# Order of the first loads, and of the MLP's products and weight sums, in a one-core hybrid decoder layer

## The chip, the cores and the metric

The kernel runs on one core of a Trainium2 chip. The metric is the device time of one launch in microseconds (us), lower is better; a time is the median of several runs. A core has five engines that work side by side and wait for each other by semaphores: TensorE (PE, matrix products; PEld is its loading of the stationary operand), VectorE (DVE), ScalarE (ACT), GpSimd (POOL) and SyncE (SP). SP, ACT and POOL also issue transfers between the chip's main memory and the on-chip memory.

## The reference

One layer: RMSNorm, one wide projection, two token mixers (pooling and a convolution) that are gated and summed, an output projection, and an MLP with a squared ReLU, all in float32.

```python
h = concat([meta, x])                       # 16 meta tokens, 256 tokens, width 2048
u = rms_norm(h, g_pre_mix)
z, v, g, gate_a, gate_b = split(u @ w_in)   # 1024, 1024, 1024, 2048, 2048 columns
y_a = multiscale_pool(z) @ w_pool_out
y_b = silu(layer_norm(depthwise_conv(v * sigmoid(g), 31 taps))) @ w_conv_out
m = sigmoid(gate_a) * y_a + sigmoid(gate_b) * y_b
h = h + rms_norm(m @ w_o, g_post_mix)
u = rms_norm(h, g_pre_mlp)
f = square(relu(u @ w_up)) @ w_down         # 2048 -> 8192 -> 2048
h = h + rms_norm(f, g_post_mlp)
return h[16:]
```

## The kernel before

**Products of split weights.** Every weight block of 1 MB (`raw`) is split into a high part, rounded by ACT (`hi`, L342, L801, L1755), and a low part, the rest, made by DVE (`lo`, L345, L806, L1760). A product takes three matmuls for each block of 128 rows (high x high, high x low, low x high). There are three buffers for high parts and three for low ones, so a weight can be split only when the product three places earlier is done. PE works through the products in a written order and never out of it.

**The start.** x lies in `x_in` (two tiles of 128 tokens), the meta tokens in `m_in`, and the first norm's weights `g_pre_mix` in 16 rows. Before anything is projected, the rows are transposed into columns (`rows_to_columns`, L407), the meta tokens are transposed in 16 pieces (`meta_tiles`, L483) and each 128 columns of x are transposed (`x_tile`, L473), scaled by ACT (L475) and split by DVE (L476). The first 512 columns of x come as two halves, one a tile, one issued by ACT and one by SP (L420). `LEAD` = 3 column blocks are turned before the first product (`acc_v`, L519). `keep_warm` (L436) fills PE with transposes of an identity whose result nobody reads: 13 ahead of the rows, 5 ahead of the first product. SP then issues the first weights in pieces, and x's further blocks between them (L337, L417).

**The MLP.** The 8192 hidden columns are done in eight pieces of 1024. Per piece there are eight products with `w_up`, called U with the half (0, 1), the pair (a, b) and the half of the depth (0, 1): U1a0 is one of them. They accumulate in banks u0 and u1, which ACT and DVE empty (`up_pair`, L1832, L1839) before relu, square and split (L1859 to L1911, tiles `F_raw` and `forms`). For `w_down`, the first seven pieces use Strassen's scheme in Winograd's form on 2 x 2 blocks: seven products P1 to P7 for one half of the output columns and seven, Q1 to Q7, for the other, in place of eight each. Four of each seven take a sum of weight blocks. P5, P6, P7 and P4 change the block B11 or B12 by adding another; Q5, Q6, Q7 and Q4 do the same with C. Before, P5, P6, Q5 and Q6 are summed by DVE from two loaded blocks (L1772, `SUM_FOR`), and P7, P4, Q7 and Q4 by a transfer that POOL issues and that adds a block from main memory onto the loaded one (L1777, `BROUGHT_FOR`). The last piece is done with eight plain products.

**Banks.** P1, P6, P7 and P4 use bank a; P5, P3 and P2 bank b; Q1, Q5, Q6 and Q7 bank x11 (its tile is `acc_up`); Q2, Q3 and Q4 have a bank each and keep their totals in it. After each of the others, `give` takes the bank's total: ACT in the first piece when it is the first to reach its place in the result (L1959), DVE otherwise (L1963). The next product in that bank waits for this.

**What sets the order.** `FIRST_PIECE`, `PIECE` and `LAST_PIECE` are strings that give PE's order of products; a + means that the product belongs to the next piece, R is a small step of the norm. A planner (`Plan`) takes the work of the other engines with assumed durations and orders each engine by due times that follow from PE's row; the order is fixed when the program is built. Seven 1 MB rooms hold loaded blocks, and `loads` issues the next load on SP whenever one is free.

Of the kernel before, what the change touches and what calls it, by code (L numbers as in the profile page):

```python
# [16 lines left out]
P = 128  # L17
# [24 lines left out]
SUMMED = {('gate0', 0): '67', ('gate0', 2): '57', ('gate1', 0): '5', ('co', 2): '46', ('o', 0): '46'}  # L42


class Plan:
# [151 lines left out]
def hybrid_block(ctx: ExitStack, tc: tile.TileContext, ins: dict, out: bass.AP):  # L197
# [217 lines left out]
    def load_x(b):  # L415
        sl = slice(b * CW, (b + 1) * CW)
        nc.sync.dma_start(x_in[:, :, sl], xv[:, :, sl])  # L417

    for t, queue in enumerate((nc.scalar, nc.sync)):
        queue.dma_start(x_in[:, t, :CW], xv[:, t, :CW])  # L420
# [139 lines left out]
    def turn_and_split(k):  # L560
        if k < KD:
            x_tile(k)
        if k == 0:
            meta_parts.pop(0)()
        pieces_to(k + 1)

    for k in range(LEAD):
        turn_and_split(k)
    keep_warm(DUMMIES[1])
    for k in range(KD):  # L570
        for j, acc in enumerate(accs):
            mm3(acc, *opened[k // HALF[0]][:2], u, (k % HALF[0], k), slice(j * P, (j + 1) * P),
# [66 lines left out]
    S1_z = Lazy("s1", [P, KP, L], "z")  # L639
# [22 lines left out]
    names_sums = [f"E{b}" for b in range(4)] + [f"O{b}" for b in range(3)]  # L662
    names_y = [f"yy{q}{l}" for q in range(KP) for l in ("", "l")]
    names_z = [f"z{q}" for q in range(KP)]
    names_s = [[f"S{b}{t}{n}" for t in range(NT) for n in range(NB)] for b in range(2)]
    names_sa = [f"sa{h}{l}" for h in range(2) for l in ("", "l")]
    names_o = [f"og{t}{n}" for t in range(NT) for n in range(NB)]
# [259 lines left out]
    def convolve(q0, nq):  # L927
        for q in on(q0, nq):
            on_scalar(T, lambda q=q: nc.scalar.activation(
                C_c()[:, q, :], A_a()[:, q, 0:T], AF.Identity, scale=taps[:, q, 0:1],  # L930
                bias=col("b_dw", q)), (f"a{q}", "taps", "vecs"), (f"c{q}",), 0.18)

        def tap(i):
            def f():
                for q in on(q0, nq):
                    nc.vector.scalar_tensor_tensor(  # L936
                        C_c()[:, q, :], A_a()[:, q, i:i + T], taps[:, q, i:i + 1], C_c()[:, q, :],
                        op0=ALU.mult, op1=ALU.add)
            return f
        for i in range(1, TAPS):  # L940
            plan.add("DVE", 0.4 * nq, tap(i), reads=[f"a{q}" for q in on(q0, nq)],
                     writes=[f"c{q}" for q in on(q0, nq)], late=0.1)

    def evac_z(q, bank):
        on_vector(L, lambda: nc.vector.tensor_mul(S1_z()[:, q, :], banks[bank][:, :L], rb),
                  (bank, "rb"), (f"z{q}",))

    def level(g):
# [6 lines left out]
    def pool(g):  # L955
        w = 1 << g
        lo_ = 2 * w - 1
        q0 = g * GK
        box = {}

        def add(j):
            def f():
                src = level(g - 1)[:, GK:, :] if g else S1_z()
                dst = level(g)
                q = j * GK
                nc.vector.tensor_add(dst[:, q:q + GK, lo_:], src[:, q:q + GK, lo_:],
                                     src[:, q:q + GK, lo_ - w:L - w])
            reads = [level_name(g - 1, j + 1)] if g else [f"z{q}" for q in on(j * GK, GK)]
            on_vector(GK * (L - lo_), f, reads, (level_name(g, j),))

        def diff():
            box["dm"] = dm = tmp.tile([P, GK, T], F32, tag="junk", bufs=1, name=f"dm_{g}")
            nc.vector.scalar_tensor_tensor(
                dm, level(g)[:, 0:GK, M:], 1.0 / (2 * w), S1_z()[:, q0:q0 + GK, M:],
                op0=ALU.mult, op1=ALU.subtract)

        def high():
            nc.scalar.copy(K0_d()[:, q0:q0 + GK, 0, :], box["dm"])

        def low():  # L980
            nc.vector.tensor_sub(K0_d()[:, q0:q0 + GK, 1, :], box["dm"],
                                 f32(K0_d()[:, q0:q0 + GK, 0, :]))
        for j in range((KP - q0) // GK):
            add(j)
            if j == 0:
                on_vector(GK * T, diff, [level_name(g, 0)] + [f"z{q}" for q in on(q0, GK)],
                          ("junk",))
                on_scalar(GK * T, high, ("junk",), (f"d{g}",))
                on_vector(GK * T, low, ("junk", f"d{g}"), (f"d{g}l",))
# [352 lines left out]
    def fu_step():  # L1342
        plan.take(form_names("fu"), names_d)
        names = [f"qu{t}{h}" for t in (1, 2) for h in (1, 2)]
        plan.take(["raw10"] + names, names_z)
# [340 lines left out]
        steps += [(s[:-1], i + 1) if s[-1] == "+" else (s, i) for s in text.split()]  # L1686
    products = [s for s in steps if s[0] != "R"]


    RAW_OF = {"1": "11", "5": "11", "6": "11", "4": "11", "3": "22", "7": "12", "2": "21"}  # L1690
    RAW_OF = {p + k: b + r for p, b in ("PB", "QC") for k, r in RAW_OF.items()}
# [161 lines left out]
    def relu_squared(h, pr, i, s_name, box):  # L1853
# [20 lines left out]
        if i < NP - 1 and h == 0:  # L1874
# [4 lines left out]
        elif i < NP - 1:  # L1879
# [11 lines left out]
        def src():  # L1891
# [5 lines left out]
        if i == NP - 1:  # L1897
            return
        if h == 0 and pr == 1:
            split_form(0, S3, "S3", S3Q, "q3")  # L1900
# [284 lines left out]
```

## Time and profile before

| | us |
|---|---|
| median of 3 runs | 1191.39 (1190.59 to 1193.03) |
| profiled execution, its own time | 1192.1 |
| its span, first to last instruction | 1190.3 |
| PE busy | 1168.5 (98%) |
| DVE busy | 1075.7 (90%) |
| ACT busy | 708.8 (60%) |
| POOL busy | 52.6 (4%) |
| PE waiting for the rows of g at the start | 3.0 |
| PE's waits in the MLP, in all | 3.5 |

A row of the timeline has the start in the span, the duration, the engine, the line, the operation, `out<-in` by the program's names, the shape and the count; in brackets the idle time before it and what ended that. SPq, ACTq and POOLq are issues of transfers. The list of waits has the engine and line, what it waited for, then total, times and longest. A group's row ends with its busy time, the mean of one in ns, and the idle time before. A transfer's row has its count, its size and the median from issue to landing.

### The profile page before, as it was taken

What the parts mean: (1) busy time and instruction counts of PE and PEld (TensorE: products, weight loads), DVE (VectorE), ACT (ScalarE), POOL (GpSimd) and SP (SyncE); (2) the same over time, 40 slices, a digit from 0 to 9 for tenths busy, and PEclk for the clock granted to TensorE, in tenths of its full rate; (3) what the DMA queues carried; (4) which work ended last, traced back from release to release, by engine and by line L of the source; (5) the groups of instructions that cost most, each with busy time, mean ns of one, the idle gap of its engine ahead of it and who ended that gap; (6) DMA issues with size and microseconds to landing.
All of it is one profiled execution on the core that took longest, in us unless ns stands there. A gap on an engine that the chain in (4) does not pass through costs nothing.

```text
span 1190.3 us, 15769 instructions
## 1 busy us (share of the span) xinstructions
PE 1168.5 (98%) x6318; PEld 1014.1 (85%) x6318; DVE 1075.7 (90%) x1160; ACT 708.8 (60%) x718; POOL 52.6 (4%) x50
## 2 busy tenths in 40 slices
PE   8999999999999999999899999999999999999996
PEld 8999998788888888898788888888888888888885
DVE  5799999999989999688988999999999999999856
ACT  6634354556379666557675665666656756656542
POOL 0000000000000000000100000000000000000000
PEclk9999999999999999999999999999999999999998
DMA  9855345799778799449898797997988987979931
GB/s 277 265 180 185 131 144 186 229 291 282 208 214 244 238 332 305 155 148 332 214 343 229 221 316 190 267 288 199 310 267 223 303 234 232 316 190 264 327 139 71
DMA packets 182457, 282.33 MB, mean 237 GB/s; under 512 B 4609, under 2 KB 92097, under 8 KB 181472
## 3 DMA queue, kind: packets, MB, share of 16 engines
q1 hardware_dynamic: 160624, 236.03, 57.7%
q0 software_dynamic: 21008, 44.04, 21.0%
q10 hardware_dynamic: 752, 1.25, 0.3%
q8 instruction: 49, 0.80, 0.3%
q14 instruction: 24, 0.20, 0.1%
HBM read 277.11 MB, written 4.19 MB: 236 GB/s over the span
## 4 chain that ended last, share of the span: by engine, by line
PE 82%; DVE 11%; DMA 4%; issue 2%; ACT 1%; DVEq 0%; ACTq 0%
PE bank_u L524 18%; PE acc_up L1934 12%; PE bank_k L1212 12%; PE bank_u L530 9%; PE bank_a L1934 7%; PE acc_v L1212 7%; PE bank_b L1934 5%; PE bank_k L519 5%; DVE lo L806 5%; DVE c L936 4%; PE acc_v L519 3%; DMA raw_k<-in_w_in_dram 2%; PE acc_up L524 1%; PE acc_v L1472 1%; PE bank_u L1934 1%
## 5 line engine op out<-in xcount | busy, mean ns | idle before, releaser
L524 PE MATMUL bank_u<-m,hi 128*128 128x512 f32 x960 | 329.6, 390 | 0.5 <-DVE F_raw L1839 0.5
L530 PE MATMUL bank_u<-m,lo 128*128 128x256 f32 x960 | 265.8, 277 | 0.0
L524 PEld LDWEIGHTS bank_u<-m,hi 128*128 128x128 f32 x960 | 180.3, 188 | 38.7 <-DVE F_raw L1839 0.8
L801 ACT CAST hi<-raw_p 128x2048 fp32r<-128x2048 f32 x70 | 133.8, 1913 | 118.0 <-PE bank_k L1212 22.6
L530 PEld LDWEIGHTS bank_u<-m,lo 128*128 128x128 f32 x960 | 180.4, 188 | 1.6
L1760 DVE TENSOR_TENSOR lo<-raw_m,hi 128x2048 fp32r<-128x2048 f32 x71 | 162.5, 2289 | 15.3 <-ACT hi L1755 15.2
L806 DVE TENSOR_TENSOR lo<-raw_p,hi 128x2048 fp32r<-128x2048 f32 x70 | 159.7, 2288 | 17.6 <-ACT hi L801 17.2
L1755 ACT CAST hi<-raw_m 128x2048 fp32r<-128x2048 f32 x71 | 135.8, 1913 | 53.2 <-PE bank_u L524 20.2
L1934 PE MATMUL acc_up<-hi,forms 128*128 128x512 f32 x440 | 143.2, 390 | 1.4 <-ACT G L1959 1.4
L1755 ACT CAST hi<-raw_h 128x2048 fp32r<-128x2048 f32 x46 | 87.9, 1912 | 47.6 <-PE bank_u L524 29.9
L1760 DVE TENSOR_TENSOR lo<-raw_h,hi 128x2048 fp32r<-128x2048 f32 x46 | 105.3, 2289 | 10.7 <-ACT hi L1755 10.7
L936 DVE SCALAR_TENSOR_TENSOR c<-a,taps,c 128x256 f32<-128x256 f32 x240 | 100.3, 480 | 0.0
L1934 PEld LDWEIGHTS acc_up<-hi,forms 128*128 128x128 f32 x440 | 82.7, 188 | 19.4 <-ACT G L1959 1.8
L519 PE MATMUL bank_k<-u_um,hi 128*128 128x272 f32 x512 | 95.2, 287 | 0.0
L1212 PE MATMUL bank_k<-hi,u_um 128*128 128x512 f32 x280 | 88.9, 390 | 0.0
L1934 PE MATMUL acc_up<-lo,forms 128*128 128x512 f32 x220 | 86.0, 391 | 0.0
L1934 PE MATMUL bank_a<-hi,forms 128*128 128x512 f32 (+1 forms) x256 | 82.1, 384 | 0.0
L519 PEld LDWEIGHTS bank_k<-u_um,hi 128*128 128x128 f32 x512 | 79.9, 189 | 0.0
L519 PE MATMUL bank_k<-u_um,lo 128*128 128x272 f32 x256 | 73.5, 287 | 0.0
L1755 ACT CAST hi<-raw_a 128x2048 fp32r<-128x2048 f32 x23 | 44.0, 1912 | 34.8 <-PE bank_u L524 25.5
L1934 PE MATMUL bank_b<-hi,forms 128*128 128x512 f32 (+1 forms) x200 | 63.5, 381 | 0.0
L1212 PEld LDWEIGHTS bank_k<-hi,u_um 128*128 128x128 f32 x280 | 52.6, 188 | 10.9
(382 smaller groups left out, 2239.3 us busy)
## 6 DMA issues: line engine op xcount, KB each, us to landing
raw_p<-in_w_in_dram SPq DMA_DIRECT2D x32, 1024.0 KB, 5.9
raw_m<-in_w_up_dram SPq DMA_DIRECT2D x25, 1024.0 KB, 9.8
raw_m<-in_w_down_dram SPq DMA_DIRECT2D x22, 1024.0 KB, 8.4
raw_h<-in_w_down_dram SPq DMA_DIRECT2D x21, 1024.0 KB, 6.0
raw_h<-in_w_up_dram SPq DMA_DIRECT2D x16, 1024.0 KB, 9.0
raw_k<-in_w_in_dram SPq DMA_DIRECT2D x12, 1024.0 KB, 8.4
raw_a<-in_w_down_dram SPq DMA_DIRECT2D x12, 1024.0 KB, 5.2
raw_a<-in_w_up_dram SPq DMA_DIRECT2D x11, 1024.0 KB
```

The costliest lines, as they stand in the source:

```text
L519: nc.tensor.matmul(acc, w[:, k[0], cs], act[:, k[1], a, off:], start=first and n == 0, stop=last and n == 2)
L524: nc.tensor.matmul(acc.rearrange("p (a t) -> p a t", a=2)[:, :, ts], hi[:, k[0], cs], act[:, k[1], :, off + ts.start:off + ts.stop], start ...
L530: nc.tensor.matmul(acc[:, :T], lo[:, k[0], cs], act[:, k[1], 0, off:], start=False, stop=stop, skip_group_check=True)
L801: nc.scalar.copy(box["flat"], rooms[q]())
L806: nc.vector.tensor_sub(lo, rooms[q](), f32(box["flat"]))
L936: nc.vector.scalar_tensor_tensor(C_c()[:, q, :], A_a()[:, q, i:i + T], taps[:, q, i:i + 1], C_c()[:, q, :], op0=ALU.mult, op1=ALU.add)
L1212: nc.tensor.matmul(banks[bank], a_(k, part), box[w_][:, k, :], start=opens and k == 0 and i == 0, stop=ends_ and k == CK - 1 and i == 2, s ...
L1472: nc.tensor.matmul(acc, act(kk)(a_, half(t)), w_[:, k, :], start=kk == 0 and n == 0, stop=kk == nk - 1 and n == 2, skip_group_check=True)
L1755: nc.scalar.copy(box["flat"], raw_in(room))
L1760: nc.vector.tensor_sub(lo, raw_in(room), f32(box["flat"]))
L1934: nc.tensor.matmul(acc, forms[h][:, f, k, a_, :], box[w_][:, k, cs], start=start and k == 0 and n == 0, stop=stop and k == KH - 1 and n == ...
```

## The change

**First loads.** The meta tokens are now SP's first transfer and the rows of g ACT's first; x's halves come second on each. The first part of the meta tokens is written (`meta_parts.pop(0)()`) before x's first tile and not after it. The transposes that nobody reads are now 11 ahead of the rows, 2 behind the meta tokens' transposes and 1 ahead of the first product.

**The MLP's order.** The first two strings are new. Which sums DVE makes is now set for each kind of piece by `PIECE_SUMS`: P5, P6, P7, Q4 and Q5 in the first piece, P5, Q5 and Q6 in the six that follow; the others are brought by a transfer. (Its third entry is for the last piece, which has no such product.)

**Without effect on the instructions.** `MOVED_TAPS` is empty, so the loop that it serves issues nothing; the tile `z` is longer, in a room that is longer still; `with_forms` says of each piece what `i < NP - 1` said.

```diff
-SUM_FOR = {"P5": ("B11", "B12"), "P6": ("B11", "B22"), "Q5": ("C11", "C12"), "Q6": ("C11", "C22")}
-BROUGHT_FOR = {"P7": ("B12", "B22"), "P4": ("B11", "B21"), "Q7": ("C12", "C22"),
-               "Q4": ("C11", "C21")}
-FIRST_PIECE = "U1a0 U1a1 R U1b0 P1 U1b1 Q1 U0a0+ U0a1+ P5 Q5 Q7 P6 U0b0+ P7 Q6 Q3 P3 P4 Q2 U0b1+ P2 Q4"
-PIECE = "U1a0 Q1 U1a1 U1b0 U1b1 P1 U0a0+ Q5 P5 U0a1+ P6 U0b0+ Q7 Q3 P7 Q6 P3 U0b1+ Q2 P4 P2 Q4"
+ADDS_FOR = {"P5": ("B11", "B12"), "P6": ("B11", "B22"), "P7": ("B12", "B22"), "P4": ("B11", "B21"),
+            "Q5": ("C11", "C12"), "Q6": ("C11", "C22"), "Q7": ("C12", "C22"), "Q4": ("C11", "C21")}
+PIECE_SUMS = ("P5 P6 P7 Q4 Q5", "P5 Q5 Q6", "P5 P6")
+FIRST_PIECE = "U1a0 U1a1 R U1b0 P1 U1b1 Q1 U0a0+ U0a1+ U0b0+ P5 Q5 P6 Q2 P7 Q3 P3 Q7 P4 U0b1+ Q6 P2 Q4"
+PIECE = "U1a0 U1a1 U1b0 U1b1 Q1 P1 U0a0+ U0a1+ Q5 P5 Q2 Q7 Q3 P6 U0b0+ Q6 P7 U0b1+ P3 Q4 P2 P4"
...
-DUMMIES = (13, 5)
+DUMMIES = (11, 2, 1)
...
+MOVED_TAPS = {}
...
+    nc.sync.dma_start(m_in, meta)
+    pre_rows = load_rows(nc.scalar, "g_pre_mix")
     for t, queue in enumerate((nc.scalar, nc.sync)):
         queue.dma_start(x_in[:, t, :CW], xv[:, t, :CW])
-    nc.sync.dma_start(m_in, meta)
-    pre_rows = load_rows(nc.scalar, "g_pre_mix")
...
-        if k == 0:
-            meta_parts.pop(0)()
         pieces_to(k + 1)
 
+    meta_parts.pop(0)()
+    keep_warm(DUMMIES[1])
     for k in range(LEAD):
         turn_and_split(k)
-    keep_warm(DUMMIES[1])
+    keep_warm(DUMMIES[2])
...
-            if s in SUM_FOR:
-                uses.append((m_, "sum", [(r, i) for r in SUM_FOR[s]]))
-            if s in BROUGHT_FOR:
-                uses.append((m_, "bring " + BROUGHT_FOR[s][1], [(BROUGHT_FOR[s][0], i)]))
+            if s in ADDS_FOR:
+                onto, what = ADDS_FOR[s]
+                if s in PIECE_SUMS[(i > 0) + (i == NP - 1)]:
+                    uses.append((m_, "sum", [(onto, i), (what, i)]))
+                else:
+                    uses.append((m_, "bring " + what, [(onto, i)]))
```

From here to the end of this section stands the order of the built instructions at three places; what a name is, is said ahead of each. The first is PE's row at the start, before:

```order
L436 MATMUL idle<-ident 128x128 x13
L407 MATMUL pv_g_pre_mix<-ident,rows_g_pre_mix 128x16
L483 MATMUL mt_in<-ident,m_in 128x16 x16
L473 MATMUL xt_172<-ident,x_in 128x128 x2
L473 MATMUL xt_181<-ident,x_in 128x128 x2
L473 MATMUL xt_188<-ident,x_in 128x128 x2
L436 MATMUL idle<-ident 128x128 x5
L519 MATMUL acc_v_0_170<-u_um,hi_83 128x272 x2
```

and with the change:

```order
L437 MATMUL idle<-ident 128x128 x11
L408 MATMUL pv_g_pre_mix<-ident,rows_g_pre_mix 128x16
L484 MATMUL mt_in<-ident,m_in 128x16 x16
L437 MATMUL idle<-ident 128x128 x2
L474 MATMUL xt_174<-ident,x_in 128x128 x2
L474 MATMUL xt_181<-ident,x_in 128x128 x2
L474 MATMUL xt_188<-ident,x_in 128x128 x2
L437 MATMUL idle<-ident 128x128
L520 MATMUL acc_v_0_168<-u_um,hi_83 128x272 x2
```

The rows of g and the meta tokens (`m_in`) keep their place ahead of x's transposes; two of the idle transposes now stand between the meta tokens and x, and one, not five, ahead of the first product.

The second is PE's row in the first piece, where Q5 ends (its weights are `hi_4855`, and `hi_4894` with the change). Before:

```order
L1934 MATMUL acc_up_3_4237<-lo_4874,forms_4476 128x512
L1934 MATMUL acc_up_3_4237<-hi_4855,forms_4476 128x512
L1934 MATMUL acc_up_3_4237<-hi_4884,forms_4476 128x512
L1934 MATMUL acc_up_3_4237<-lo_4914,forms_4476 128x512
L1934 MATMUL acc_up_3_4237<-hi_4884,forms_4476 128x512 x2
```

and with the change:

```order
L1965 MATMUL acc_up_3_4233<-lo_4915,forms_4472 128x512
L1965 MATMUL acc_up_3_4233<-hi_4894,forms_4472 128x512
L1965 MATMUL bank_a<-hi_4929,forms_4473 128x512
L1965 MATMUL bank_a<-lo_4934,forms_4473 128x512
```

Before, Q7 opened the bank that Q5 had filled, `acc_up_3`, right behind it; now P6 follows, in bank a.

The third is DVE's row in the second piece, from the taking of P3's total on (`bank_b`) to the low part of P2's weights, before:

```order
L1963 TENSOR_TENSOR F_raw<-F_raw,bank_b 128x512
L1760 TENSOR_TENSOR lo_5698<-raw_h_4596,hi_5694 128x2048
L1877 TENSOR_TENSOR F_raw<-F_raw 128x256
L1963 TENSOR_TENSOR G<-G,acc_up_3_4237 128x512
L1839 TENSOR_TENSOR F_raw<-half_2_5716,bank_u_4486 128x256
L1760 TENSOR_TENSOR lo_5738<-raw_c,hi_5733 128x2048
```

and with the change, from the low part of Q4's weights (`lo_5713`) over that of P2's (`lo_5733`) to that of P4's (`lo_5751`):

```order
L1994 TENSOR_TENSOR G<-G,acc_up_3_4233 128x512
L1791 TENSOR_TENSOR lo_5713<-raw_h_4592,hi_5690 128x2048
L1870 TENSOR_TENSOR F_raw<-half_2_5711,bank_u_4482 128x256
L1791 TENSOR_TENSOR lo_5733<-raw_m_4480,hi_5727 128x2048
L1994 TENSOR_TENSOR F_raw<-F_raw,bank_b 128x512
L1791 TENSOR_TENSOR lo_5751<-raw_h_4592,hi_5747 128x2048
```

P3's total was taken ahead of P2's low part and now stands behind it. `L1870` and `L1839` empty a bank of U.

More of the change, by code (lines that the diff above doesn't have):

```diff
@@ L638, in hybrid_block @@
     K0_h1 = Lazy("k8", [P, NT, D], "h1", bufs=2)
-    S1_z = Lazy("s1", [P, KP, L], "z")
+    S1_z = Lazy("s1", [P, KP * L + 3 * 2 * T], "z")
     S1_q = Lazy("s1", [P, 2, CK * CW], "q_u")
@@ L664, in hybrid_block @@
     names_z = [f"z{q}" for q in range(KP)]
+    names_w = [f"w{j}{e}" for j in range(3) for e in range(2)]
     names_s = [[f"S{b}{t}{n}" for t in range(NT) for n in range(NB)] for b in range(2)]
@@ L939, in tap, with scaled, z_view, w_view @@
             return f
-        for i in range(1, TAPS):
+        def scaled(i, j, q):
+            nc.scalar.activation(w_view(j)[:, q - q0, :], A_a()[:, q, i:i + T], AF.Copy,
+                                 scale=taps[:, q, i:i + 1])
+        moved = MOVED_TAPS.get(q0 // nq, 0)
+        for i in range(1, 1 + moved):
+            j = w_next[0] % 3
+            w_next[0] += 1
+            for q in on(q0, nq):
+                on_scalar(T, lambda i=i, j=j, q=q: scaled(i, j, q), (f"a{q}", "taps"),
+                          (f"w{j}{q - q0}",), 0.18)
+            names = [f"c{q}" for q in on(q0, nq)]
+            plan.add("POOL", 1.27, lambda j=j: nc.gpsimd.dma_start(
+                C_c()[:, q0:q0 + nq, :], w_view(j), accum_op=ALU.add),
+                reads=[f"w{j}{e}" for e in range(nq)] + names, writes=names)
+        for i in range(1 + moved, TAPS):
             plan.add("DVE", 0.4 * nq, tap(i), reads=[f"a{q}" for q in on(q0, nq)],
                      writes=[f"c{q}" for q in on(q0, nq)], late=0.1)
+    w_next = [0]
+    def z_view():
+        return S1_z()[:, :KP * L].rearrange("p (q l) -> p q l", l=L)
+    def w_view(j):
+        return S1_z()[:, KP * L + j * 2 * T:KP * L + (j + 1) * 2 * T].rearrange(
+            "p (q t) -> p q t", t=T)
     def evac_z(q, bank):
-        on_vector(L, lambda: nc.vector.tensor_mul(S1_z()[:, q, :], banks[bank][:, :L], rb),
+        on_vector(L, lambda: nc.vector.tensor_mul(z_view()[:, q, :], banks[bank][:, :L], rb),
                   (bank, "rb"), (f"z{q}",))
@@ L962, in f @@
             def f():
-                src = level(g - 1)[:, GK:, :] if g else S1_z()
+                src = level(g - 1)[:, GK:, :] if g else z_view()
                 dst = level(g)
@@ L1344, in fu_step @@
         names = [f"qu{t}{h}" for t in (1, 2) for h in (1, 2)]
-        plan.take(["raw10"] + names, names_z)
+        plan.take(["raw10"] + names, names_z + names_w)
         q_u = {f"{t + 1}{h + 1}": (lambda t=t, h=h: S1_q()[:, 0, (t * 2 + h) * CW:
@@ L1687, in hybrid_block, with with_forms @@
     products = [s for s in steps if s[0] != "R"]
+    def with_forms(i):
+        return any(s[0] == "P" and k == i for s, k in products)
     RAW_OF = {"1": "11", "5": "11", "6": "11", "4": "11", "3": "22", "7": "12", "2": "21"}
@@ L1873, in relu_squared @@
         plan.add("ACT", 0.53, square, reads=(s_name,), writes=(s_name,), late=0.1)
-        if i < NP - 1 and h == 0:
+        if with_forms(i) and h == 0:
             plan.add("ACT", 0.32, lambda: nc.scalar.copy(q_(S1Q), a_(A2)),
@@ L1878, in relu_squared @@
                      reads=(s_name,), writes=(f"q3{pr}",), late=0.1)
-        elif i < NP - 1:
+        elif with_forms(i):
             plan.add("DVE", 0.35, lambda: nc.vector.tensor_sub(q_(S1Q), q_(S1Q), a_(A2)),
@@ L1896, in relu_squared @@
                  reads=(s_name, A), writes=(A + "l",), late=0.1)
-        if i == NP - 1:
+        if not with_forms(i):
             return
```

2 lines of the change are left out of this document (1 added, 1 removed).

## The prediction

> **What bounds the kernel now.** I read the page's busy table and the shares of its chain of waits first, then the list of what TensorE (PE) waited for.
>
> ```profile
> PE 1168.5 (98%) x6318; PEld 1014.1 (85%) x6318; DVE 1075.7 (90%) x1160; ACT 708.8 (60%) x718; POOL 52.6 (4%) x50
> ...
> PE 82%; DVE 11%; DMA 4%; issue 2%; ACT 1%; DVEq 0%; ACTq 0%
> ```
>
> ```profile
> PE pv_g_pre_mix L407 <- DMA rows_g_pre_mix<-in_g_pre_mix_dram: 3.0, 1, 3.0
> PE acc_v L1212 <- ACT sg L1261: 1.9, 1, 1.9
> PE bank_b L1934 <- DVE lo L1760: 1.6, 1, 1.6
> PE acc_up L1934 <- ACT G L1959: 1.4, 1, 1.4
> ...
> PE bank_u L524 <- DVE F_raw L1839: 0.5, 1, 0.5
> ```
>
> PE holds 82% of the chain that ended last and is idle for 1190.3 - 1168.5 = 21.8 us. The change leaves every product in place, so it can win only idle time, and can lose without limit by making more. Two of its parts touch rows of this list: the start (3.0, for a load) and the first piece of the MLP (1.6, 1.4 and 0.5). Then I cut the span into stretches; the columns are the length, then busy time (and count) of PE, PEld, DVE, ACT, POOL, then clock, DMA share, GB/s.
>
> ```profile
> 7.40:11.60 4.20, 4.16 (x28) 4.12 (x29) 1.60 (x6) 1.51 (x5) 0.00 (x0) 1.00 1.06 368
> ...
> 650.00:732.00 82.00, 82.00 (x427) 70.22 (x426) 77.79 (x66) 51.98 (x45) 5.13 (x4) 1.00 0.90 256
> 732.00:814.00 82.00, 82.00 (x427) 70.27 (x426) 77.79 (x66) 51.95 (x45) 5.13 (x4) 1.00 0.90 257
> ```
>
> The equal counts of the last two rows show the MLP's period: one piece takes 82 us and has four accumulating transfers. There PE is busy 82.00 of 82.00. So the middle pieces have nothing to give: freeing DVE (77.79 of 82) is worth nothing there, and all the new order can do in them is harm.
>
> **The start.** Before, g's rows and the meta tokens stand behind x's halves on their queues, but PE's own order wants them first.
>
> ```profile
> 0.73 0.41 ACTq L420 DMA_DIRECT2D x_in<-in_x_dram  x1
> ...
> 1.36 3.04 PE L436 MATMUL idle<-ident 128*128 128x128 f32 x13 [1.36 <-POOL ident masks.py:199]
> ...
> 7.44 0.28 PE L407 MATMUL pv_g_pre_mix<-ident,rows_g_pre_mix 16*128 16x16 f32 x1 [3.05 <-DMA rows_g_pre_mix<-in_g_pre_mix_dram]
> ...
> 7.57 1.86 PE L483 MATMUL mt_in<-ident,m_in 16*128 16x16 f32 x16
> ...
> 9.36 1.54 PE L473 MATMUL xt<-ident,x_in 128*128 128x128 f32 x6
> ...
> 10.46 0.34 ACT L492 CAST u_um<-mt 128x192 fp32r<-128x192 f32 x1
> ...
> 10.70 1.27 PE L436 MATMUL idle<-ident 128*128 128x128 f32 x5
> 10.70 0.41 ACT L342 CAST hi<-raw 128x256 fp32r<-128x256 f32 x1
> ...
> 11.62 0.80 PE L519 MATMUL acc_v<-u_um,hi 128*128 128x272 f32 x2
> ...
> 12.90 0.31 PE L519 MATMUL acc_v<-u_um,lo 128*128 128x272 f32 x1
> 13.05 0.38 PE L473 MATMUL xt<-ident,x_in 128*128 128x128 f32 x2
> ...
> 14.03 0.38 PE L473 MATMUL xt<-ident,x_in 128*128 128x128 f32 x2
> ```
>
> ```profile
> x_in<-in_x_dram SPq DMA_DIRECT2D x3, 512.0 KB, 6.7
> ...
> raw_p<-in_w_o_dram POOLq DMA_DIRECT2D x1, 1024.0 KB, 12.0
> ...
> out_dram<-F_raw ACTq DMA_DIRECT2D x1, 320.0 KB, 2.5
> x_in<-in_x_dram ACTq DMA_DIRECT2D x1, 256.0 KB, 5.3
> ```
>
> x was there at 0.73 + 5.3 = 6.0 and waited until 9.36 behind 16 meta transposes. Issued first (136 KB in all), rows and meta land between 0.73 + 2.5 = 3.2 (the shortest landing of a transfer of that order) and 6.0 (when 512 KB in the same place had landed); I take 5.0. The 11 dummies end at 4.40 - 2 x 0.21 = 4.0, the rows' transpose and the meta tiles take 1.99 (7.44 to 9.43), two dummies 0.43: PE is at the first x transpose at 7.4 (5.6 to 8.4). x's halves, now behind 136 KB and 0.45 us of issue, land between 6.0 + 136/368 = 6.4 and 7.4, by when all four were in before. So that transpose starts at 7.4 (6.4 to 8.4). From it to the first product it took 11.62 - 9.36 = 2.26; four of the five dummies go (4 x 0.21 = 0.84), and the 0.34 us cast of the meta part, now done in the wait, stood ahead of the first weight's cast, which ended at 11.11, 1.75 after the transpose. Without it, and with 0.2 to start, that is about 1.6. First product at 9.0 (8.0 to 10.0): 2.6 earlier.
>
> Its cover: the loads of k run ahead. x's next block, issued at 3.06, lands at 9.8, and the transpose that wants it, at 14.03 before, would come at 11.4. A k step takes 14.03 - 13.05 = 0.98 us of PE. No later wait of PE is on a load, so DVE, ACT and the rooms they free move along with it.
>
> What I can't see is the clock. The first six matmuls of a product start over 12.90 - 11.62 = 1.28, 0.26 apart, while a whole later step of six and two transposes takes 0.98: PE ran at half rate until about 12.9. If full rate now comes before the first product, the gain is 0.65 more, half of 1.28. If it comes at 12.9 as before, 2.6 us more of products at half rate cost half of that, 1.3. So the start's gain lies between 1.6 - 0.8 = 0.8 and 3.6 + 0.65 = 4.3; I take 2.6, in the middle. [...]
>
> **The first piece.** These rows carry its two larger waits, and DVE's durations; the third fence is grouped over 650 to 1113.
>
> ```profile
> 573.89 2.29 DVE L1760 TENSOR_TENSOR lo<-raw_c,hi 128x2048 fp32r<-128x2048 f32 x1 [0.18 <-ACT hi L1755]
> ...
> 576.24 0.50 PE L1934 MATMUL bank_b<-lo,forms 128*128 128x512 f32 x1 [1.64 <-DVE lo L1760]
> ...
> 582.51 0.59 ACT L1959 ACTIVATE G<-acc_up 128x512 f32<-128x512 f32 x1
> ...
> 583.15 0.50 PE L1934 MATMUL acc_up<-hi,forms 128*128 128x512 f32 x1 [1.40 <-ACT G L1959]
> ...
> 586.00 0.39 PE L1934 MATMUL bank_a<-hi,forms 128*128 128x512 f32 x1
> ...
> 588.72 0.40 PE L524 MATMUL bank_u<-m,hi 128*128 128x512 f32 x1
> ```
>
> ```profile
> 628.67 2.29 DVE L1772 TENSOR_TENSOR raw_m<-raw_m,raw_h 128x2048 f32<-128x2048 f32 x1 [1.51 <-DMA raw_h<-in_w_down_dram]
> ...
> 630.88 2.29 DVE L1760 TENSOR_TENSOR lo<-raw_a,hi 128x2048 fp32r<-128x2048 f32 x1
> ```
>
> ```profile
> L1839 DVE TENSOR_TENSOR F_raw<-half,bank_u 128x256 f32<-128x256 f32 x44 | 18.4, 418 | 2.3 <-ACT half L1832 2.2
> ...
> L1963 DVE TENSOR_TENSOR F_raw<-F_raw,bank_b 128x512 f32<-128x512 f32 x17 | 11.6, 685 | 0.0
> ```
>
> A P or Q product takes 588.72 - 586.00 = 2.72, so a U product (82 - 14 x 2.72)/8 = 5.5. The 1.64 is P5 reaching its low weights before DVE made them. Now U0b0 stands ahead of P5: 5.5 us more for DVE, which owes there only the sum for P5 and one more low part, 2 x 2.29. I count it all won. The 1.40 is Q7 opening the bank that Q5 had just left, until ACT emptied it; now six products stand between them, 6 x 2.72 at least. Won too. The 0.5 came of a DVE sum held 1.51 by a load, with the emptying of a U bank behind it; sums still wait for loads, so I count 0.3 (0 to 0.5). Together 3.3.
>
> Elsewhere in the table: 28 DVE sums become 5 + 6 x 3 = 23 and 28 accumulating transfers 33, so a middle piece frees 2.29 us of DVE and adds one transfer of 1 MB. The `with_forms`, tap and view edits give the same instructions.
>
> What the middle pieces may lose: P3 and P2 share bank b. Before, U0b1, Q2 and P4 stood between them; now only Q4. P2 may open the bank when DVE has taken P3's total, and DVE's order has the low parts of Q4 and of P2, and an emptying, ahead of that: 2.29 + 0.42 + 2.29 + 0.69, less three overlaps of 0.08 (628.67 to 630.88 is 2.21 for 2.29) = 5.45, against 2 x 2.72 = 5.44 for P3 and Q4. So P2 waits for as long as DVE starts Q4's low part late, and behind P2 stands the whole row of PE. Below: 0. Above: 1.5 a piece, the 1.51 that DVE was once held. With PE never waiting in the pieces of before, I take 0.05, six times: 0.3.
>
> **Sum.** The profiled execution took 1192.1 (span 1190.3 and 1.8 around it): 1192.1 - 2.6 - 3.3 + 0.3 = 1186.5. It lay 0.7 above the median of 1191.39, so 1185.8.
>
> **Rivals.** (1) The bank wait recurs: DVE is late by 0.6 a piece, 6 x 0.6 = 3.6 in place of 0.3: 1189.1. For it: 5.45 against 5.44. Against: DVE gets 2.29 us a piece back.
>
> (2) Slower: the transfers become the bound. In the piece from 650 to 732:
>
> ```profile
> DMA  9950077999999969599999999999887089999659
> ...
> q1 hardware_dynamic: 12544, 16.78, 59.8%
> q0 software_dynamic: 2089, 4.15, 29.8%
> ...
> raw_m<-in_w_down_dram POOLq DMA_DIRECT2D x2, 1024.0 KB, 9.3
> ```
>
> Four accumulations take 29.8% of 82, 6.1 each; a fifth brings 0.90 to 0.97. Q4's weights are now such a sum, and their landing starts the chain of P2. If they take 12.0 (the longest row of all such transfers) and not 9.3, and nothing hides the 2.7, that is 16.2 in place of 0.3: 1201.7. From (2.6 + 3.3)/6 = 1.0 us a piece on it makes the change a loss. Against it: the zeros in the slices, where nothing moves for lack of rooms.
>
> (3) The start wins nothing, since x lands late and the clock stays low: 1185.8 + 2.6 = 1188.4.
>
> **Chances.** Forecast 0.66, (1) 0.16, (2) 0.10, (3) 0.08. The range, 1182.5 to 1190.0, takes in the start's 4.3 and the first rival, and leaves out the second. What can be told from no change is about 0.2%, 2.4 us: faster is below 1189.0. The forecast gives nearly all of its 0.66 to faster, (1) about 0.07 and (3) 0.06: 0.79. Same: 0.12. Slower: 0.09, nearly all from (2).
>
> **What would show it.** Right: first L520 product near 9.0, the rows' transpose near 5, no wait over 0.5 on banks b or x11 between 545 and 650, and 82.0 a piece. Wrong: PE waits on DVE at bank_b once a piece; landings of POOL's transfers near 12; an x transpose that waits beyond 8.4; a period over 82.6.

## The result, and the profile after

The change makes the kernel slower: 1200.3 us median (1199.14 to 1201.27, 4 runs) for 1191.05 of before (1190.59 to 1193.03, 4 runs). The ratio is 1.0074, with a 95% interval from 1.0057 to 1.0092, so some 9 us. The forecast was 1185.8 us, and the time lies outside its range. The profiled execution took 1200.04 us (span 1198.2; before 1190.3).

First the busy table's row of the engines, then the list of TensorE's waits (total, times, longest), all of the changed kernel.

```profile
PE 1172.8 (98%) x6314; PEld 1014.8 (85%) x6314; DVE 1062.9 (89%) x1155; ACT 708.9 (59%) x718; POOL 59.0 (5%) x55
```

```profile
PE acc_up L1965 <- DVE lo L1791: 5.0, 5, 1.6
PE bank_b L1965 <- DVE F_raw L1994: 3.1, 6, 1.0
PE acc_v L1238 <- ACT sg L1287: 1.9, 1, 1.9
PE bank_k L520 <- DVE lo L808: 1.8, 1, 1.8
...
PE bank_k L520 <- ACT hi L803: 0.4, 1, 0.4
PE pv_g_pre_mix L408 <- DMA rows_g_pre_mix<-in_g_pre_mix_dram: 0.2, 1, 0.2
```

Read it against the list of before. The waits that the change aimed at are gone: 3.0 for g's rows is 0.2, and the 1.6, 1.4 and 0.5 of the first MLP piece do not appear. In their place stand two new ones in the middle pieces (acc_up five times, bank_b six times, 8.1 us in all) and two at the start of the mixer (bank_k, 2.2 us). DVE is less busy than before, as planned, and it bought nothing. The list counts only idle time. The matmuls right behind a wait also start up to 0.34 us apart instead of 0.23, so a wait costs more than its entry; what each part costs in full is worked out at the end of the section on the prediction.

The stretches say where. Columns: length, TensorE's busy time and matmuls, granted clock, share of the transfer engines, GB/s. First two of before, then after:

```profile
222.00:226.00 4.00, 3.53 (x15) 1.00 0.93 296
...
550.00:650.00 100.00, 96.46 (x498) 1.00 0.93 263
```

```profile
30.00:34.00 4.00, 1.83 (x14) 0.93 1.09 352
34.00:38.00 4.00, 4.00 (x24) 0.65 1.10 350
222.00:226.00 4.00, 2.94 (x10) 0.82 0.85 269
226.00:230.00 4.00, 4.00 (x15) 0.75 0.70 255
550.00:650.00 100.00, 100.00 (x523) 1.00 0.88 259
732.00:814.00 82.00, 80.74 (x417) 1.00 0.94 265
```

Three facts. The first piece (550 to 650) now has no gap at all, where the same stretch of before was 96.46 busy: 3.5 us of idle won, for the forecast's 3.3. A middle piece that was 82.00 of 82.00 now has 80.74 in this one, and 80.0 to 81.6 in the six. And behind the new wait at 31 to 34 us the clock falls: 0.07 x 4 and 0.35 x 4 are 1.68 us of lost clock, which is 3.4 us at half speed (from 34 to 36 us the granted clock is 0.50). The same follows the wait of 1.88 at 223 us (0.18 x 4 and 0.25 x 4, 1.72 us; 0.50 from 225 to 227); that wait was there before too (1.86), but the clock stayed at 1.00 behind it.

**The start.** TensorE's first rows in the timeline of after:

```profile
4.16 0.28 PE L408 MATMUL pv_g_pre_mix<-ident,rows_g_pre_mix 16*128 16x16 f32 x1 [0.20 <-DMA rows_g_pre_mix<-in_g_pre_mix_dram]
...
6.57 1.49 PE L474 MATMUL xt<-ident,x_in 128*128 128x128 f32 x6
...
8.06 0.82 PE L520 MATMUL acc_v<-u_um,hi 128*128 128x272 f32 x2
...
9.46 0.33 PE L520 MATMUL acc_v<-u_um,lo 128*128 128x272 f32 x1
9.63 0.38 PE L474 MATMUL xt<-ident,x_in 128*128 128x128 f32 x2
...
31.22 0.52 PE L520 MATMUL bank_k<-u_um,hi 128*128 128x272 f32 x2 [0.36 <-ACT hi L803]
33.55 0.59 PE L520 MATMUL bank_k<-u_um,lo 128*128 128x272 f32 x1 [1.81 <-DVE lo L808]
```

The first product starts at 8.06 instead of 11.62, 3.56 earlier, more than the forecast's 2.6. Its first six matmuls start over 1.40 us (8.06 to 9.46) where the next six take 0.70 (9.77 to 10.47), so at half rate as in before (1.28 and then 0.71), and the next x transpose is at 9.63 instead of 13.05: full rate came 3.4 us earlier as well, and 3.4 of the lead are left. Then, at 31 us, the next weights (`raw_s0a`) are missing. The row of ScalarE that casts them, in before and in after:

```profile
29.47 1.91 ACT L801 CAST hi<-raw_s0a 128x2048 fp32r<-128x2048 f32 x1 [1.20 <-DMA raw_s0a<-in_w_in_dram]
```

```profile
29.26 1.90 ACT L803 CAST hi<-raw_s0a 128x2048 fp32r<-128x2048 f32 x1 [4.41 <-DMA raw_s0a<-in_w_in_dram]
```

The load lands at nearly the same moment (casts at 29.47 and 29.26), though TensorE is ahead. Before, ScalarE waited 1.20 us for it and TensorE did not notice; with its lead, TensorE runs into it.

**The middle pieces.** POOL issues the accumulating transfers, five a piece. Three of its rows after (the sums of P6, P4 and Q4) and, a piece later, that of P6 again, and the rows that follow for ScalarE, VectorE and TensorE:

```profile
739.06 1.28 POOL L1808 DMA_DIRECT2D raw_m<-in_w_down_dram  x1 [11.37 <-DVE lo L1791]
753.15 1.28 POOL L1808 DMA_DIRECT2D raw_m<-in_w_down_dram  x1 [12.81 <-DVE lo L1791]
758.48 1.28 POOL L1808 DMA_DIRECT2D raw_h<-in_w_down_dram  x1 [4.05 <-DVE lo L1791]
...
822.61 1.28 POOL L1808 DMA_DIRECT2D raw_m<-in_w_down_dram  x1 [11.37 <-DVE lo L1791]
```

```profile
772.25 1.91 ACT L1786 CAST hi<-raw_h 128x2048 fp32r<-128x2048 f32 x1 [5.30 <-DMA raw_h<-in_w_down_dram]
...
774.19 2.29 DVE L1791 TENSOR_TENSOR lo<-raw_h,hi 128x2048 fp32r<-128x2048 f32 x1 [3.88 <-ACT hi L1786]
776.40 0.41 DVE L1870 TENSOR_TENSOR F_raw<-half,bank_u 128x256 f32<-128x256 f32 x1
...
776.54 0.50 PE L1965 MATMUL acc_up<-lo,forms 128*128 128x512 f32 x1 [0.82 <-DVE lo L1791]
...
776.73 2.29 DVE L1791 TENSOR_TENSOR lo<-raw_m,hi 128x2048 fp32r<-128x2048 f32 x1
778.93 0.68 DVE L1994 TENSOR_TENSOR F_raw<-F_raw,bank_b 128x512 f32<-128x512 f32 x1
...
779.76 0.47 PE L1965 MATMUL bank_b<-hi,forms 128*128 128x512 f32 x1 [0.43 <-DVE F_raw L1994]
```

From 739.06 to 822.61 is one piece: 83.55 us for 82. The transfer issued at 758.48 is Q4's sum (raw_h). It lands 13.7 us later; ScalarE waits 5.30 for it, VectorE 3.88, TensorE at Q4's low weights (0.82 at acc_up). Then the very chain that the prediction wrote down runs, late: low part of Q4, an emptying, low part of P2, P3's total, and P2 waits for bank b. So the two waits of a piece have one origin.

### The profile page after: what moved, and what is told of

Same layout as the page of the kernel before. It is cut to its first block, busy times and chain, and to the rows that moved or that the text cites. A ratio compares the mean times of both kernels' runs of the same rounds, so it can differ in the third digit from the quotient of the medians.

```text
span 1198.2 us, 15790 instructions
## 1 busy us (share of the span) xinstructions
PE 1172.8 (98%) x6314; PEld 1014.8 (85%) x6314; DVE 1062.9 (89%) x1155; ACT 708.9 (59%) x718; POOL 59.0 (5%) x55
## 5 line engine op out<-in xcount | busy, mean ns | idle before, releaser
L1786 ACT CAST hi<-raw_m 128x2048 fp32r<-128x2048 f32 x69 | 132.0, 1913 | 62.0 <-PE bank_u L525 31.5
L1791 DVE TENSOR_TENSOR lo<-raw_m,hi 128x2048 fp32r<-128x2048 f32 x69 | 157.8, 2289 | 9.6 <-ACT hi L1786 9.3
L1791 DVE TENSOR_TENSOR lo<-raw_h,hi 128x2048 fp32r<-128x2048 f32 x52 | 119.1, 2290 | 30.1 <-ACT hi L1786 30.0
L1786 ACT CAST hi<-raw_h 128x2048 fp32r<-128x2048 f32 x52 | 99.5, 1914 | 62.5 <-DMA raw_h<-in_w_down_dram 26.3
L1965 PEld LDWEIGHTS acc_up<-hi,forms 128*128 128x128 f32 x440 | 82.6, 188 | 17.5
L1791 DVE TENSOR_TENSOR lo<-raw_a,hi 128x2048 fp32r<-128x2048 f32 x21 | 48.1, 2290 | 11.7 <-ACT hi L1786 11.7
```

What stands on the lines that cost most here:

```text
L1786: nc.scalar.copy(box["flat"], raw_in(room))
L1791: nc.vector.tensor_sub(lo, raw_in(room), f32(box["flat"]))
L1965: nc.tensor.matmul(acc, forms[h][:, f, k, a_, :], box[w_][:, k, cs], start=start and k == 0 and n == 0, stop=stop and k == KH - 1 and n == ...
```

## The experiments

Each kernel was timed beside runs of before on its own chip (medians of before 1191.6, 1192.5 and 1191.8 in the three groups). Only the ratio with its interval is compared; in us it is taken times 1192. Groups one and two ask what each part of the change does, group three whether the reasons hold.

**The start alone.** The diff to before is the change's load order, the meta part ahead of the loop, and the dummies:

```diff
-DUMMIES = (13, 5)
+DUMMIES = (11, 2, 1)
...
+    nc.sync.dma_start(m_in, meta)
+    pre_rows = load_rows(nc.scalar, "g_pre_mix")
     for t, queue in enumerate((nc.scalar, nc.sync)):
         queue.dma_start(x_in[:, t, :CW], xv[:, t, :CW])
-    nc.sync.dma_start(m_in, meta)
-    pre_rows = load_rows(nc.scalar, "g_pre_mix")
```

> The start of the change alone, with the old product rows and the old choice of sums in every MLP piece. The forecast's step: the lead of the first product moves through to the end, 2.6 us faster (about 1188.5 for 1191.1). [...] If the lead comes through, the cause of the loss lies in the MLP alone.

Measured: 1191.13 us, ratio 1.0000 (0.9988 to 1.0011). Nothing is won, against the forecast's 2.6. The row of ScalarE and the stretch of TensorE in this kernel:

```profile
28.74 1.91 ACT L803 CAST hi<-raw_s0a 128x2048 fp32r<-128x2048 f32 x1 [3.45 <-DMA raw_s0a<-in_w_in_dram]
```

```profile
30.00:34.00 4.00, 2.73 (x24) 2.27 (x22) 2.59 (x2) 3.50 (x5) 0.00 (x0) 1.00 1.09 349
34.00:38.00 4.00, 4.00 (x35) 4.00 (x34) 2.80 (x4) 3.94 (x8) 0.00 (x0) 1.00 1.09 349
```

The wait for raw_s0a is there (1.3 us), but this execution kept its full clock behind it (1.00, where the change has 0.93 and 0.65), so the slow clock is not certain to follow. The author's estimate from the change's trace, about 1193 with the wait and the slow clock both coming again, was too pessimistic. The wait by itself does not use up the lead: this execution still ends 2.0 us ahead of before's (span 1188.3 for 1190.3). The mean granted clock of its 12 runs goes from 0.997 (1190.1 to 1191.3 us) to 0.992 (1194.2 us), and the four at 0.994 or less took 1193.1 to 1195.0. So the nothing of the median is the wait, and in some executions a slower clock; how much of it is the clock is not shown.

**The first piece alone**, with the old start and the old middle:

```diff
-FIRST_PIECE = "U1a0 U1a1 R U1b0 P1 U1b1 Q1 U0a0+ U0a1+ P5 Q5 Q7 P6 U0b0+ P7 Q6 Q3 P3 P4 Q2 U0b1+ P2 Q4"
+FIRST_PIECE = "U1a0 U1a1 R U1b0 P1 U1b1 Q1 U0a0+ U0a1+ U0b0+ P5 Q5 P6 Q2 P7 Q3 P3 Q7 P4 U0b1+ Q6 P2 Q4"
...
+PIECE_SUMS = ("P5 P6 P7 Q4 Q5", "P5 P6 Q5 Q6", "P5 P6")
```

> The first MLP piece's new row and sums alone, with the old start and the old middle pieces. The forecast's step and the reading of the traces agree on 3.3 to 3.6 us faster (about 1187.6): the waits of 1.64, 1.40 and 0.5 us in that piece go and nothing takes their place. Rival: the waits only move into the second piece, since its first weights are then needed sooner; then less than 1 us is won and the second piece shows a new wait.

Measured: 1187.81 us, ratio 0.9963 (0.9951 to 0.9975), 4.4 us faster (3.0 to 5.8). Its stretch from 550 to 650 is 100.00 busy and the next, from 650 to 732, 82.00: nothing moved on.

**The middle pieces alone**, with the old start and first piece:

```diff
-PIECE = "U1a0 Q1 U1a1 U1b0 U1b1 P1 U0a0+ Q5 P5 U0a1+ P6 U0b0+ Q7 Q3 P7 Q6 P3 U0b1+ Q2 P4 P2 Q4"
+PIECE = "U1a0 U1a1 U1b0 U1b1 Q1 P1 U0a0+ U0a1+ Q5 P5 Q2 Q7 Q3 P6 U0b0+ Q6 P7 U0b1+ P3 Q4 P2 P4"
...
+PIECE_SUMS = ("P5 P6 Q5 Q6", "P5 Q5 Q6", "P5 P6")
```

> The middle pieces' new row and sums alone, with the old start and the old first piece. The forecast's step: 0.3 us slower in all (about 1191.4), at most 1.5 us for each of the six pieces. The reading of the traces: 8 to 9 us slower (about 1199.5), as 0.6 us for each piece at bank_b (P2 behind P3) and 0.7 to 1.8 us at acc_up behind Q4's late low weights. Rival, that the middle pieces lose only because the changed start or first piece puts them out of step with their loads: no more than 2 us slower.

Measured: 1203.42 us, ratio 1.0089 (1.0073 to 1.0105), 10.6 us slower (8.7 to 12.5). The loss is in the middle pieces by themselves, so it does not need the other two parts. The three parts alone add up to 0 - 4.4 + 10.6 = 6.2; the change whole is 8.8 (6.8 to 11). With the intervals of all four, the difference is not clear of noise.

**Taps in two loads**, in the whole change. Among the loads ahead of raw_s0a on its queue is taps_in, 31 rows of 4 KB; between the two stand only the five small ones of `load_rows`. The share of the transfer engines in after, in one microsecond (the column before the last):

```profile
26.00:27.00 1.00, 1.00 (x10) 1.00 0.07 13
```

A share of 0.07 is about one engine of 16 (0.0625) while raw_s0a, issued at 16.59, is still owed. That it is the 31 rows that hold this one engine is the author's reading of the row; this run tests it.

```diff
-    nc.sync.dma_start(taps_in, w_dw)
+    for t in (slice(0, 16), slice(16, TAPS)):
+        nc.sync.dma_start(taps_in[t, :], w_dw[t, :])
```

> The change whole, but the load of taps_in (31 rows of 4 KB) is issued as 16 and 15 rows instead of as one. Theory: the one load of 31 rows runs on one transfer engine alone (the share of transfer engines is 0.07 between 26 and 27 us, which is one of 16), and raw_s0a, queued behind it, lands when that engine is done. Split in two, raw_s0a lands near 26 instead of 29.3, TensorE does not wait between 31 and 34 us, keeps its full clock there, and the run is 3.5 to 5 us faster than the change (about 1196). Rival: raw_s0a is late because all engines are full with the weights ahead of it; then the split does nothing, and the run stays at 1200.

Measured: 1198.54 us, ratio 1.0053 (1.0039 to 1.0067), beside the change's 1.0074. In its trace (its lines stand one lower from here on) the weights are there when ScalarE comes to them, with no wait in the row:

```profile
24.89 1.91 ACT L804 CAST hi<-raw_s0a 128x2048 fp32r<-128x2048 f32 x1
```

The share of the transfer engines from 26 to 27 us is 1.09 for the 0.07, and TensorE is busy 4.00 of 4.00 from 30 to 34 us, at clock 1.00. The reason holds, and the rival fails: nothing ahead of raw_s0a was taken away. The size, 2.5 us by the two ratios, is less than the 3.5 to 5 expected, and the two intervals overlap; a pair of kernels further down (the start without and with the split) shows the same 2.5, with intervals that only touch.

**Only the sums of the middle pieces**, old row:

```diff
+PIECE_SUMS = ("P5 P6 Q5 Q6", "P5 Q5 Q6", "P5 P6")
```

> The old start, first piece and product row of the middle pieces; only the choice of sums in the middle pieces is the new one, so that P6's sum comes by an accumulating transfer instead of an add on VectorE. Theory of the transfers (five instead of four accumulating transfers in a piece make every one of them late): most of the loss of the middle pieces is here already, 5 to 12 us slower than before, with waits on late low weights. Theory of the row (Q4's weights are wanted early behind P3, and P2 shares P3's bank with one product between): within 1 us of before, TensorE without a gap in the middle pieces.

Measured: 1202.9 us, ratio 1.0096 (1.0077 to 1.0115). The theory of the row fails here: a fifth transfer hurts the old row by itself. The waits are others than in the change:

```profile
PE bank_a L1965 <- DVE lo L1791: 2.7, 6, 0.5
...
PE bank_u L525 <- DVE F_raw L1870: 2.3, 4, 0.6
```

bank_a is P6, whose sum is now brought with only U0a1 between P5 and P6. The transfer behind one of these waits (issued at 737.88) is not slow and has no other near it (POOL's rows in the middle pieces stand 10.6 us apart or more). It lands in 8.5 us, and ScalarE is already waiting for it:

```profile
746.45 1.91 ACT L1786 CAST hi<-raw_c 128x2048 fp32r<-128x2048 f32 x1 [0.26 <-DMA raw_c<-in_w_down_dram]
```

So here a product follows too soon even for a transfer that has no other accumulating one beside it. The listed waits come to 5.0 of 11.4 us, but the list counts idle time alone: from 737.88 to 822.15 (POOL's row of P6's sum in this piece and the next) a piece takes 84.3 us, for 81.8 in before (744.27 to 826.11), so the loss is in the middle pieces.

**Only the row of the middle pieces**, old sums (P5, P6, Q5 and Q6 on VectorE, four transfers a piece, as before):

```diff
+PIECE_SUMS = ("P5 P6 Q5 Q6", "P5 P6 Q5 Q6", "P5 P6")
```

> The old start, first piece and choice of sums; only the product row of the middle pieces is the new one, P6's sum is again an add on VectorE. Theory of the row: 6 to 12 us slower than before, with the bank_b wait of P2 (0.6 us a piece) and the wait behind Q4's low weights (0.7 to 1.8 a piece) both there. Theory of the transfers: the wait behind Q4 goes, because its transfer has one less to share with, the bank_b wait stays, 3 to 4 us slower. If neither wait shows, the two parts of the change hurt only together.

Measured: 1210.42 us, ratio 1.0148 (1.0127 to 1.0169), 17.6 us slower, the slowest of all, with no more transfers than before. That is more than either theory had, and it needs no fifth transfer. Its list has both waits:

```profile
PE acc_up L1965 <- DVE lo L1791: 8.1, 10, 1.3
PE bank_b L1965 <- DVE F_raw L1994: 3.9, 6, 1.8
```

The ten at acc_up are two kinds. One is Q4's, as in the change (1.33 at 783.52). The other is Q2's, right behind P5 (0.55 at 751.54): VectorE had P6's sum to add just ahead (2.29 from 746.99), which the change leaves to a transfer. So the 17.6 us are not all of Q4's making. POOL's rows, and the landing of the second one (last column, us):

```profile
759.58 1.28 POOL L1808 DMA_DIRECT2D raw_a<-in_w_down_dram  x1 [26.62 <-DVE lo L1791]
764.92 1.28 POOL L1808 DMA_DIRECT2D raw_m<-in_w_down_dram  x1 [4.05 <-DVE lo L1791]
```

```profile
raw_m<-in_w_down_dram POOLq DMA_DIRECT2D x1, 1024.0 KB, 14.2
```

Again two transfers 5.3 us apart, again one that takes 14 us. They are P4's and Q4's: in the new row only U0b0 stands between P6 and Q6, whose low weights release them. In before the nearest two of POOL's rows in the middle pieces, with the old row, are these, 12.4 us apart:

```profile
878.14 1.28 POOL L1777 DMA_DIRECT2D raw_a<-in_w_down_dram  x1 [31.57 <-ACT hi L1755]
890.54 1.28 POOL L1777 DMA_DIRECT2D raw_m<-in_w_down_dram  x1 [11.12 <-ACT half L1832]
```

**Q4's sum on VectorE**, new row, old start and first piece:

```diff
-PIECE_SUMS = ("P5 P6 Q5 Q6", "P5 Q5 Q6", "P5 P6")
+PIECE_SUMS = ("P5 P6 Q5 Q6", "P5 Q5 Q6 Q4", "P5 P6")
```

> The middle pieces' new row and sums with the old start and first piece, but Q4's sum is an add on VectorE (2.7 us a piece there) instead of an accumulating transfer. Theory, that Q4's transfer lands late: the wait behind Q4's low weights (6.1 us in all in the kernel with the middle pieces alone) goes and the bank_b wait of P2 stays, so 3 to 5 us slower than before instead of 12. Rival, that VectorE's row of work is what is late there and not the transfer: the add puts 2.7 us more ahead of the same low weights, the wait grows, 12 us slower or more.

Measured: 1191.42 us, ratio 0.9992 (0.9980 to 1.0004). VectorE's sums of two blocks take 2.29 us each in before and in after, not 2.7. The whole loss is gone, not two thirds of it, and a middle piece is full again:

```profile
732.00:814.00 82.00, 82.00 (x427) 1.00 0.91 257
```

No bank_b wait behind VectorE's totals is left in its list. So that wait followed from Q4's late weights; P3 and P2 with one product between them cost nothing by themselves. Another close pair stays in this kernel (806.19 and 811.08, the landings of raw_c, which has the later one, at a median of 11.8), without a wait of TensorE: being late cost nothing where the product follows later.

**P4's sum on VectorE**, Q4's by transfer as in the change:

```diff
-PIECE_SUMS = ("P5 P6 Q5 Q6", "P5 Q5 Q6", "P5 P6")
+PIECE_SUMS = ("P5 P6 Q5 Q6", "P5 Q5 Q6 P4", "P5 P6")
```

> The old start and first piece, the new row in the middle pieces, Q4's sum by a transfer as in the change, but P4's sum by an add on VectorE. Theory of the overlap: in the change P4's and Q4's transfers are issued 5.3 us apart and share the transfer engines, so that Q4's takes 13.7 us; alone it lands in some 9.2 us, the wait behind Q4's low weights falls to 0.3 us a piece or less, the bank_b wait, which follows from it, goes as well, and the run is within 2 us of before. Theory of the distance: Q4 stands too close behind Q6, whose weights it adds to, for any transfer to land in time; then the waits stay, 6 us slower than before or more.

Measured: 1191.74 us, ratio 0.9996 (0.9987 to 1.0005). Q4's place is the same as in the change, and its transfer too; only P4's is gone from beside it. Its row and its landing:

```profile
760.92 1.28 POOL L1808 DMA_DIRECT2D raw_m<-in_w_down_dram  x1 [17.96 <-DVE lo L1791]
```

```profile
raw_m<-in_w_down_dram POOLq DMA_DIRECT2D x1, 1024.0 KB, 9.1
```

9.1 us for 13.7, and no wait. The distance from Q6 to Q4 was enough for a transfer that has no other beside it. This is the run that separates overlap from distance: it has the row of the kernel that lost 17.6 us and as many transfers (four a piece), and only the close pair is gone. How two of them slow each other, on the transfer engines or in POOL's queue, no run separates; the earlier one of the pair takes longer too (11.7 us in the change, at 753.15).

**Taps in two loads alone, and with the start.** Both have the old rows and sums.

> The kernel before, with nothing but taps_in loaded as 16 and 15 rows. Theory: raw_s0a lands near 26 instead of 29.5, but TensorE wants its low part at 34.6 and has it at 33.7 already, so nothing is won: within 1 us of before, and ScalarE's wait of 1.2 us for raw_s0a gone. If more than 1.5 us is won, the weights were on the path already before the change.

Measured: 1191.57 us, ratio 0.9994 (0.9985 to 1.0002): nothing, as expected. In before the load was late for ScalarE only.

> The change's start alone (old rows and sums in all MLP pieces) with taps_in loaded as 16 and 15 rows. Theory: of the lead of 3.6 us at the first product nearly all comes through to the end, 2.5 to 3.5 us faster than before (about 1189). If the lead is taken by a later wait as well, less than 1 us, as with the start alone.

Measured: 1189.34 us, ratio 0.9979 (0.9970 to 0.9988), 2.5 us faster (1.4 to 3.6). With the taps split most of the lead comes through; without it, nothing does on the median (1.0000). The stretch of this kernel at the place where the transfer engines stood idle:

```profile
26.00:27.00 1.00, 1.00 (x10) 1.00 1.09 349
```

**The parts that win, together.** First the start with split taps and the first piece, old middle; then the whole change with split taps and Q4's sum on VectorE. The diff is that of the second, against the change:

```diff
-PIECE_SUMS = ("P5 P6 P7 Q4 Q5", "P5 Q5 Q6", "P5 P6")
+PIECE_SUMS = ("P5 P6 P7 Q4 Q5", "P5 Q5 Q6 Q4", "P5 P6")
...
-    nc.sync.dma_start(taps_in, w_dw)
+    for t in (slice(0, 16), slice(16, TAPS)):
+        nc.sync.dma_start(taps_in[t, :], w_dw[t, :])
```

> The change's start with taps_in loaded as 16 and 15 rows, and the change's first MLP piece, with the old row and sums in the middle pieces: the parts that the runs so far show to win, together. Expected: the first piece's 3.8 us as measured alone, and of the lead of 3.6 us at the start some 2.5 to 3.3 that now come through, about 1185 for 1191.5. If the lead is lost again at a later wait, 1187.5, as with the first piece alone.

Measured: 1184.7 us, ratio 0.9941 (0.9927 to 0.9954).

> The whole change with the two mends that the runs point to: taps_in loaded as 16 and 15 rows, and Q4's sum in the middle pieces an add on VectorE. If the runs so far have found all that the change loses, it is as fast as the change's start and first piece with the old middle (1184.7 for 1192.5, 7.8 us faster than before), perhaps 1 us faster still. If the new middle row loses once its first piece is the new one, 1188 or more.

Measured: 1183.94 us (1182.69 to 1184.93), ratio 0.9932 (0.9919 to 0.9946), 8.1 us faster than before (6.4 to 9.7). This is the change mended in two places, and it beats both kernels. Its whole list of waits of TensorE:

```profile
PE acc_v L1239 <- ACT sg L1288: 2.1, 1, 2.1
PE idle L438 <- POOL ident masks.py:199: 1.4, 1, 1.4
PE acc_v L521 <- DVE y L1060: 0.4, 1, 0.4
```

Whether the new middle row is worth anything over the old one is not settled: 0.9932 and 0.9941 overlap.

## Why the prediction was wrong

**The start: the mechanism right, the cover wrong.** Rows at 4.16 (forecast 5.0), first transpose at 6.57 (7.4), first product at 8.06 (9.0): each earlier than predicted. So the third rival had its reason wrong (x did not land late); that the start alone wins nothing came about in another way. Full rate came 3.4 us earlier (9.63 for 13.05), along with the work, which is neither of the two cases that the prediction set bounds by; what sets that moment, no run shows. The step that failed is "No later wait of PE is on a load, so DVE, ACT and the rooms they free move along with it". It was read from the list of TensorE's waits, which names the last releaser only. One engine further back, before's ScalarE row of 29.47 has its 1.20 us on raw_s0a: that load came at a time that TensorE's lead hardly moved (casts at 29.47, 29.26 and 28.74), with little slack behind it (29.47 + 1.91 + 2.29 = 33.7 for the low weights, which TensorE wanted at 34.6). A lead of 3.4 us is more than that slack of 0.9, so most of it meets the load. The runs put the term at 0 (start alone) and at 2.5 when the taps' load no longer holds raw_s0a, close to the forecast's 2.6.

**The first piece: right.** Forecast 3.3, measured 4.4 (3.0 to 5.8), all three waits gone, none behind them. That it is more than the 3.5 of idle fits the slow matmuls behind each wait (0.33 us apart behind the 1.64 and the 1.40, for 0.23).

**The middle pieces: the step that decided.** "I take 0.05, six times: 0.3", with 1.5 a piece as the upper end. The measured loss is 10.6 in the part alone, 1.8 a piece over six (1.45 to 2.1), at or above that bound. The arithmetic of the chain (5.45 against 5.44) was sound, and with Q4 or P4 on VectorE TensorE shows no wait there. What failed is its start: it took VectorE's start of Q4's low part as late by at most 1.51, the longest that a load had held it before; in the change VectorE sits idle 3.88 ahead of it. Nothing in the forecast's sum asked when Q4's transfer would be issued and which other transfer would be under way then (P4's, 5.3 us ahead of it). Both follow from the row: the distance from P6 to Q6 fixes the spacing of two transfers. Three of the prediction's signs of being wrong came: bank_b once a piece, a landing past 12, and a period over 82.6 (83.55).

**The rivals.** The first (bank wait of 0.6 a piece) named a wait that came, 3.1 us over six pieces, but as a consequence; alone it does not exist. The second came close in time (1201.7 for 1200.3) and in its price, Q4's transfer at 12.0 instead of 9.3 and 2.7 a piece; measured are 13.7 and some 1.8. That the time came so close is partly luck, since it counts 2.6 for the start, which came to nothing. And it tied the price to the fifth transfer and the share of 0.97. With four transfers the row alone loses 17.6 us, and the row with P4's sum taken off loses none: in this row it is two transfers at once, not how many a piece. In the old row a fifth one does cost 11.4 us, but because P6 follows it too soon and not because it lands late (8.5). At 0.10 it had far too small a chance; its argument against, the zeros in the engines' slices, speaks of the mean over a piece and not of the one moment that counts.

**In the profiled execution** the parts can be read off three matmuls that both kernels have in the same place: `bank_b<-diag,ones` in the step R (546.26 in before, 547.42 in after), the first of P1 in the second piece (646.75 and 643.67) and the first in bank a of the last piece (1145.93 and 1153.80). So after is 1.2 us behind when the first piece starts: the lead of 3.4 and 1.2 more are lost, at raw_s0a and at 223 us with the slow clock behind both. It is 3.1 ahead behind the first piece (4.2 won), and 7.9 behind when the middle pieces are done: they cost 10.9 here, of which the list of waits shows 8.1. The difference of the spans is 7.9 as well. The two stretches of slow clock belong to this execution (mean granted clock 0.994); the four timed runs lie between 0.993 and 0.996.

## What to carry to other kernels

Before counting a lead as won, look one engine further back than the waiting one: a load that any engine waits for, even for 1 us and off the path (1.20 here), may come at a time that the lead does not move, and then stops whoever arrives earlier. When a row of products is rearranged and some weights are summed by transfers, list when each transfer can be issued (behind the last reader of what it adds to) and keep two of them further apart than one takes to land, unless the later product is far off: here two 5.3 us apart made TensorE wait, where one alone landed in 9.1. A small load of an awkward shape ahead of a large one is worth a look: here splitting one in two was worth 2.5 us.

## What the runs showed of the hardware

- With the load of 31 rows ahead of raw_s0a on its queue, the share of the transfer engines fell to 0.07 from 26 to 27 us, about one engine of 16, and raw_s0a, a 1 MB load, came late: its cast starts at 29.26 in the change, behind a wait of 4.41. With the 31 rows as 16 and 15 the share in the same microsecond is 1.09, and the cast starts at 24.89 without a wait.
- Two accumulating transfers of 1 MB were issued 5.3 us apart: the later took 13.7 us (in the change) and 14.2 (with the row alone) instead of 9.1 (with P4's sum on VectorE).
- Behind a wait of TensorE of 1.88 us the granted clock was at half for 3.4 us (0.50 from 225 to 227 us, in after), and behind one of 2.7 at the same product it fell too (the first piece alone, 0.69 from 222 to 226 and 0.89 from 226 to 230). Behind 1.86 us in before, 2.10 us in the kernel with both mends and 2.62 us with the old middle it did not, clock 1.00 behind all three. So in these executions the length of the wait does not tell whether the slow clock follows; what does, no run here was made to show.
